# The output gates of a hybrid encoder kernel: GpSimd taken out, bound and negation on VectorE, three ScalarE functions in a row

## The chip, the cores and the metric

The kernel runs on one core of one Trainium2 chip. Its time is the device time of one execution in microseconds (us); runs are compared by their median. TensorE (PE) multiplies matrices, VectorE (DVE) and ScalarE (ACT) work on tiles of 128 partitions, GpSimd (POOL) is the fourth compute engine, and SyncE (SP) issues the transfers. Each engine works its own list of instructions in order; semaphores make it wait for the others.

## The reference, cut to what matters

Two layers of an encoder run over 272 positions (256 tokens and 16 meta tokens) of width 2048. Each layer has one wide input projection, a bidirectional gated linear attention (GLA) with 4 heads, a neighbourhood attention (NA) with 16 heads, an output projection and a squared-ReLU MLP. The part that matters here is the output gate of the GLA heads: a quarter of the projection's GLA columns, `r`, goes through `silu` and multiplies the normalised attention output.

```python
    o = o * lax.rsqrt(jnp.mean(jnp.square(o), axis=-1, keepdims=True) + LN_EPS) * norm_w.astype(f32)
    o = o.reshape(B, L, GLA_HEADS * GLA_DV) * jax.nn.silu(r.astype(f32))
    return o.astype(q.dtype)
```

`silu(r)` is r / (1 + exp(-r)).

## The kernel before, in words

Activations lie transposed: a tile has 128 features on the partitions and the positions along the free side (272 in layer 0; the last layer needs 256 for the gates). Every product is made of fp32r parts. A weight chunk of 128x1024 lands in `raw`, ScalarE rounds it to `wh` (L165), VectorE forms the rest `wl` = raw - wh (L166), and TensorE multiplies wh and wl with the high and low halves of the activations: three matmuls of 272 columns for each of 16 row blocks in layer 0 (L178, L179, L180), or a 512- and a 256-column one in layer 1 (L174, L175). So a gate tile takes 48 matmuls in layer 0 and 32 in layer 1. Three chunk buffers are in turn, and the chunks of the whole kernel stream through them.

`by_m` runs one output tile after the other: it fills a PSUM bank `mm`, hands it to an eviction function, and calls `pump` twice a tile. Where the bank holds 256 + 256 columns (layer 1), `whole` first joins the two halves into the SBUF tile `jn` (a ScalarE copy, L187, and a VectorE add, L188), and the eviction reads that.

`pump` moves side work along. Side work stands in two queues of Python generators, `fg` and `bg`; a step runs a generator up to its next `yield`, and its VectorE instructions may not stand ahead of the newest `wl`. In the gate stage each pump gives one step of `fg` and 1.3 of `bg`. In `bg` are the four GLA heads. A head has nine levels of scores: VectorE forms `dif` (L494), ScalarE takes exponentials into `lev` (L496, L498), VectorE multiplies by q and k (L499), TensorE makes the scores into a bank `bg` (L520), VectorE merges them by a mask (L527). Then follow one more product (L535), the product with V (L553 to L557), a mean of squares (L560, L227, L791), its Newton step, and at the end the output `on`, which is multiplied by the gate tiles (L572, L573) and split into `y`. In `fg` are the gates' later steps and, from the next stage on, the NA pairs (scores L613, transposes L649, outputs L664).

The order on each engine is laid down by the tile framework's scheduler when the program is built: it takes instructions by priority when its own model of time says they are ready, so a change of one instruction can move others. That order is fixed before the run.

The gates: `ev_r` evicts each of 8 gate tiles a layer. ScalarE writes exp(-r) from the bank into `rs` (L442); GpSimd adds one (L443); ScalarE writes -r into `rv` (L445). The generator `silu` then lets two steps pass, takes Ln and Exp (L454, L455) in its third, which gives a first value of 1 / (1 + exp(-r)), and at the next VectorE does one Newton step and the product (L457, L458, L459). `rs` and `rv` have two buffers each. A head's end waits until its two gate tiles are there.

Of the kernel before, what the change touches and what calls it, by code (L numbers as in the profile page):

```python
# [10 lines left out]
AF = mybir.ActivationFunctionType  # L11
ALU = mybir.AluOpType
# [41 lines left out]
class Trunk:  # L54
# [382 lines left out]
    def ev_r(self, c, ps):  # L437

        nc, n = self.nc, self.n
        self.y[c] = self.pair(self.yp, "y", c)  # L440
        s = self.g2.tile([P, L], F32, name="rs", tag="rs")[:, :n]
        nc.scalar.activation(s, ps, AF.Exp, scale=-1.0)  # L442
        nc.gpsimd.tensor_scalar(s, s, 1.0, 1.0, ALU.mult, ALU.add)  # L443
        r = self.g2.tile([P, L], F32, name="rv", tag="rv")[:, :n]
        nc.scalar.mul(r, ps, -1.0)  # L445
        self.fg.append(self.silu(c, s, r))

    def silu(self, c, s, r):
        nc = self.nc
        stt = nc.vector.scalar_tensor_tensor  # L450
        yield
        yield
        gate = self.g2.tile([P, L], F32, name=f"gate{c}", tag=f"gate{c}", bufs=1)[:, :self.n]
        nc.scalar.activation(gate, s, AF.Ln)  # L454
        nc.scalar.activation(gate, gate, AF.Exp, scale=-1.0)  # L455
        yield
        stt(s, s, 1e30, gate, ALU.min, ALU.mult)  # L457
        stt(s, s, 2.0, gate, ALU.subtract, ALU.mult)  # L458
        nc.vector.tensor_tensor(gate, r, s, ALU.mult)  # L459
        self.gate[c] = gate  # L460
# [692 lines left out]
```

## Time and profile before

| | us |
|---|---|
| median of 3 runs (2367.51 to 2368.08) | 2367.93 |
| the profiled execution: its time | 2367.06 |
| the profiled execution: its span, first to last instruction | 2365.3 |
| gate stage of layer 0, first and last L442 | 117.2, 170.5 |
| gate stage of layer 1, first and last L442 | 1326.2, 1380.3 |

The profile is that of one execution. An engine's busy time is the time in which it has an instruction in work; an idle stretch is put down to what came last before it ended. In rows of a window, x is the number of instructions; in rows of the timeline, the columns are start, duration, engine, line, operation, output and input, and in brackets the idle time just before and what ended it.

### The profile page before, as it was taken

Reading aid. Unit: us, or ns where it says so; the run is one execution under the profiler, and the core shown is the slowest. Engines: PE = TensorE matmul, PEld = TensorE weight load, DVE = VectorE, ACT = ScalarE, POOL = GpSimd, SP = SyncE. Lnnn points to the kernel's source line nnn. Section 1 sums busy time; section 2 is a strip of 40 time slices with the busy share of each in tenths; the row PEclk is TensorE's granted clock in tenths of the full one; section 3 lists DMA queues with packets and bytes.
Section 4 is the critical chain, followed back from the end, with each engine's and each line's share of the span. In section 5 each row is a group of like instructions: output and inputs, shape, how many; then the busy total and the mean of one; then the engine's idle time right before and its main releaser. Section 6 shows DMA issues by size and latency. Waiting matters only on the chain.

```text
span 2365.3 us, 43178 instructions
## 1 busy us (share of the span) xinstructions
PE 2340.4 (99%) x17354; PEld 2228.3 (94%) x17354; DVE 1568.2 (66%) x2458; ACT 1240.6 (52%) x2267; POOL 124.5 (5%) x197
## 2 busy tenths in 40 slices
PE   9999999999999999999999999999999999999997
PEld 9999999999999999999999899998988888888887
DVE  6687777785544455547577887768866555666656
ACT  6566665564433344444456767655654333444444
POOL 1110000020000000000021010000200000000001
PEclk9999999999999999999999999999999999999999
DMA  7544445555555555555555454546566666666664
GB/s 250 167 140 143 140 145 160 179 179 179 179 180 182 182 179 178 180 180 178 180 179 182 151 158 144 154 152 202 185 194 195 193 193 194 196 192 193 195 192 138
DMA packets 120424, 417.47 MB, mean 177 GB/s; under 512 B 13404, under 2 KB 18396, under 8 KB 120224
## 3 DMA queue, kind: packets, MB, share of 16 engines
q1 hardware_dynamic: 120224, 414.72, 56.1%
q8 instruction: 136, 2.23, 0.4%
q14 instruction: 64, 0.52, 0.1%
HBM read 412.57 MB, written 2.10 MB: 175 GB/s over the span
## 4 chain that ended last, share of the span: by engine, by line
PE 93%; DVE 4%; issue 1%; ACT 1%; POOL 0%; DMA 0%; SPq 0%; ACTq 0%; DVEq 0%; POOLq 0%
PE mm L174 21%; PE mm L178 17%; PE mm L179 17%; PE mm L180 17%; PE mm L175 11%; PE mm L204 6%; PE bg L520 1%; DVE wl L166 1%; PE bg L664 1%; ACT wh L165 0%; PE bg L613 0%; PE bg L351 0%; PE mm L946 0%; PE bg L553 0%; PE mm L961 0%
## 5 line engine op out<-in xcount | busy, mean ns | idle before, releaser
L166 DVE TENSOR_TENSOR wl<-raw,wh 128x1024 fp32r<-128x1024 f32 (+1 forms) x764 | 931.6, 1220 | 642.3 <-ACT wh L165 629.4
L165 ACT CAST wh<-raw 128x1024 fp32r<-128x1024 f32 (+1 forms) x764 | 796.4, 1042 | 926.6 <-PE mm L179 368.5
L178 PE MATMUL mm<-x,wh 128*128 128x272 f32 (+2 forms) x2176 | 622.4, 286 | 0.0
L179 PE MATMUL mm<-x,wh 128*128 128x272 f32 (+2 forms) x2176 | 617.9, 284 | 0.0
L180 PE MATMUL mm<-x,wl 128*128 128x272 f32 (+2 forms) x2176 | 617.0, 284 | 0.1
L179 PEld LDWEIGHTS mm<-x,wh 128*128 128x128 f32 x2176 | 408.7, 188 | 0.1
L178 PEld LDWEIGHTS mm<-x,wh 128*128 128x128 f32 x2176 | 407.6, 187 | 1.1 <-issue 0.5
L180 PEld LDWEIGHTS mm<-x,wl 128*128 128x128 f32 x2176 | 407.2, 187 | 0.5 <-DVE wl L166 0.5
L174 PE MATMUL mm<-x,wh 128*128 128x512 f32 x1152 | 397.6, 391 | 0.0
L175 PE MATMUL mm<-x,wl 128*128 128x256 f32 x1152 | 318.1, 276 | 0.0
L174 PEld LDWEIGHTS mm<-x,wh 128*128 128x128 f32 x1152 | 216.3, 188 | 45.0 <-issue 0.6
L174 PE MATMUL mm<-y,wh 128*128 128x512 f32 x672 | 230.3, 388 | 0.0
L175 PEld LDWEIGHTS mm<-x,wl 128*128 128x128 f32 x1152 | 216.2, 188 | 0.0
L178 PE MATMUL mm<-y,wh 128*128 128x272 f32 x704 | 199.2, 283 | 0.0
L179 PE MATMUL mm<-y,wh 128*128 128x272 f32 x704 | 199.2, 283 | 0.0
L180 PE MATMUL mm<-y,wl 128*128 128x272 f32 x704 | 199.0, 283 | 0.0
L175 PE MATMUL mm<-y,wl 128*128 128x256 f32 x672 | 184.6, 275 | 0.7 <-DVE wl L166 0.7
L174 PE MATMUL mm<-u,wh 128*128 128x512 f32 x480 | 164.7, 388 | 0.0
L174 PEld LDWEIGHTS mm<-y,wh 128*128 128x128 f32 x672 | 126.0, 188 | 26.0 <-ACT wh L165 0.2
L178 PE MATMUL mm<-u,wh 128*128 128x272 f32 x512 | 144.9, 283 | 0.0
L179 PE MATMUL mm<-u,wh 128*128 128x272 f32 x512 | 144.9, 283 | 0.0
L180 PE MATMUL mm<-u,wl 128*128 128x272 f32 x512 | 144.7, 283 | 0.0
(264 smaller groups left out, 3285.5 us busy)
## 6 DMA issues: line engine op xcount, KB each, us to landing
raw<-in_wff SPq DMA_DIRECT2D x512, 512.0 KB, 3.5
raw<-in_win SPq DMA_DIRECT2D x190, 512.0 KB, 3.6
raw<-in_wout SPq DMA_DIRECT2D x64, 512.0 KB, 3.5
nb<-in_nab SPq DMA_DIRECT2D x16, 352.0 KB, 3.5
xraw<-in_xT SPq DMA_DIRECT2D x7, 272.0 KB, 5.1
out<-acc SPq DMA_DIRECT2D x7, 256.0 KB, 2.4
wraw<-in_wup SPq DMA_DIRECT2D x2, 392.0 KB
raw<-in_win SPq DMA_DIRECT2D x4, 128.0 KB, 2.7
```

The lines of the kernel that those rows point to most:

```text
L165: nc.scalar.copy(wh[:, c], raw[:, c])
L166: self.wl = nc.vector.tensor_tensor(wl[:, c], raw[:, c], wh[:, c].bitcast(F32), ALU.subtract).ins
L174: mm(ps, lhsT=wh[:, c:c + P], rhs=x.joined, start=first, stop=False)
L175: mm(ps[:, T:], lhsT=wl[:, c:c + P], rhs=xh[:, :T], start=False, stop=last)
L178: mm(o, lhsT=wh[:, c:c + P], rhs=xh[:, :n], start=first, stop=False)
L179: mm(o, lhsT=wh[:, c:c + P], rhs=xl[:, :n], start=False, stop=False)
L180: mm(o, lhsT=wl[:, c:c + P], rhs=xh[:, :n], start=False, stop=last)
L204: self.nc.tensor.matmul(ps[m][:, :n], lhsT=parts[p][0][:, c:c + P], rhs=acts[j][parts[p][1]][:, :n], start=j + p == 0, stop=j == nk - 1 an ...
L520: nc.tensor.matmul(ps[:, b], lhsT=k[:, b], rhs=q[:, r], start=True, stop=True)
L664: nc.tensor.matmul(r[hs], lhsT=(v2 if rest else v1)[:, t, hs], rhs=p2[:, t, :] if rest else p1[:, 2 * t + hh, :], start=rest, stop=not rest)
```

## The change

```diff
@@ ev_r
         s = self.g2.tile([P, L], F32, name="rs", tag="rs")[:, :n]
-        nc.scalar.activation(s, ps, AF.Exp, scale=-1.0)
-        nc.gpsimd.tensor_scalar(s, s, 1.0, 1.0, ALU.mult, ALU.add)
         r = self.g2.tile([P, L], F32, name="rv", tag="rv")[:, :n]
-        nc.scalar.mul(r, ps, -1.0)
+        nc.vector.tensor_scalar(r, ps, -1.0, 85.0, ALU.mult, ALU.min)
+        nc.scalar.activation(s, r, AF.Exp)
         self.fg.append(self.silu(c, s, r))
@@ silu
-        yield
-        yield
         gate = self.g2.tile([P, L], F32, name=f"gate{c}", tag=f"gate{c}", bufs=1)[:, :self.n]
-        nc.scalar.activation(gate, s, AF.Ln)
+        nc.scalar.activation(gate, s, AF.Ln, bias=self.one)
         nc.scalar.activation(gate, gate, AF.Exp, scale=-1.0)
         yield
-        stt(s, s, 1e30, gate, ALU.min, ALU.mult)
+        stt(s, s, 1.0, gate, ALU.add, ALU.mult)
         stt(s, s, 2.0, gate, ALU.subtract, ALU.mult)
         nc.vector.tensor_tensor(gate, r, s, ALU.mult)
```

VectorE now evicts the tile: it negates r and bounds it at 85 (L443 of the changed file), from the bank in layer 0 and from `jn` in layer 1. ScalarE takes exp of that (L444), then Ln with a bias of one (L451), then Exp (L452). The Newton step adds the one itself (L454 to L456). A gate takes one step of `fg` where it took three, two of them empty; its VectorE part runs at the start of the step that follows. From L445 of the old file on, a line has a number lower by 3 in the changed one: L520 is L517, L499 is L496, L494 is L491.

The first place is in layer 0, after the sixth gate tile, where head 0 ends and head 1 forms its first level. VectorE before (`on` and `y` end head 0; `dif`, `lev` with `_85`, `_81` belong to head 1):

```order
L573 TENSOR_TENSOR on<-on,gate_1617 128x272
L573 TENSOR_TENSOR on<-on,gate_1771 128x272
L166 TENSOR_TENSOR wl<-raw,wh 128x1024
L227 TENSOR_TENSOR y_1518<-on,y_1518 128x272
L227 TENSOR_TENSOR y_1611<-on,y_1611 128x272
L494 TENSOR_TENSOR dif<-be_85 128x2x256
L166 TENSOR_TENSOR wl<-raw,wh 128x1024
L499 TENSOR_TENSOR lev<-lev,qk_81 128x2x256
```

VectorE now, at the same place:

```order
L570 TENSOR_TENSOR on<-on,gate_1523 128x272
L570 TENSOR_TENSOR on<-on,gate_1621 128x272
L454 SCALAR_TENSOR_TENSOR rs<-rs,gate_2017 128x272
L227 TENSOR_TENSOR y_1518<-on,y_1518 128x272
L455 SCALAR_TENSOR_TENSOR rs<-rs,gate_2017 128x272
L227 TENSOR_TENSOR y_1616<-on,y_1616 128x272
L456 TENSOR_TENSOR gate_2017<-rv,rs 128x272
L166 TENSOR_TENSOR wl<-raw,wh 128x1024
L491 TENSOR_TENSOR dif<-be_85 128x2x256
L166 TENSOR_TENSOR wl<-raw,wh 128x1024
L443 TENSOR_SCALAR rv<-mm 128x272
L496 TENSOR_TENSOR lev<-lev,qk_81 128x2x256
```

The three gate operations of the sixth tile, which stood behind this `lev`, are ahead of it, and so is the eviction of the seventh tile; the eviction of the sixth (another L443) stands three rows above the piece. ScalarE at that place, before:

```order
L442 ACTIVATE rs<-mm 128x272
L445 ACTIVATE rv<-mm 128x272
L454 ACTIVATE gate_2371<-rs 128x272
L226 CAST y_1518<-on 128x272
L226 CAST y_1611<-on 128x272
L455 ACTIVATE gate_2371<-gate_2371 128x272
L165 CAST wh<-raw 128x1024
```

ScalarE now:

```order
L444 ACTIVATE rs<-rv 128x272
L451 ACTIVATE gate_2017<-rs,one 128x272
L452 ACTIVATE gate_2017<-gate_2017 128x272
L226 CAST y_1518<-on 128x272
L226 CAST y_1616<-on 128x272
L165 CAST wh<-raw 128x1024
```

The second read of the bank is gone, and the three functions follow each other. On TensorE the scores that use this `lev` stood two matmuls into the eighth gate tile and now stand 16 into it, so 14 matmuls later.

The second place is the same one in layer 1. TensorE before (x_13030 is the fourth row block of the eighth gate tile; L520 with `qk` is the diagonal level):

```order
L174 MATMUL mm<-x_12989,wh 128x512
L175 MATMUL mm<-x_12989,wl 128x256
L174 MATMUL mm<-x_13030,wh 128x512
L520 MATMUL bg<-lev 128x128 x2
L520 MATMUL bg<-lev,qk_14504 128x128 x2
L175 MATMUL mm<-x_13030,wl 128x256
```

TensorE now (x_13559 is the ninth row block):

```order
L174 MATMUL mm<-x_13427,wh 128x512
L175 MATMUL mm<-x_13427,wl 128x256
L174 MATMUL mm<-x_13559,wh 128x512
L517 MATMUL bg<-lev 128x128 x2
L517 MATMUL bg<-lev,qk_14496 128x128 x2
L175 MATMUL mm<-x_13559,wl 128x256
```

Head 1's first scores of layer 1 stand 10 matmuls later, its next levels 10 to 24 later; from head 2 on most of them are where they were. Elsewhere, the first NA pair of each layer starts two tiles (96 matmuls in layer 0) earlier, since `fg` is empty sooner, the next pairs by less, and the fifth where it did.

## The prediction

> **What bounds the kernel now.** I read the busy times and the chain of the page first, then the windows around the two gate stages, then each wait of TensorE in them.
>
> ```profile
> span 2365.3 us, 43178 instructions
> ...
> PE 2340.4 (99%) x17354; PEld 2228.3 (94%) x17354; DVE 1568.2 (66%) x2458; ACT 1240.6 (52%) x2267; POOL 124.5 (5%) x197
> ...
> PE 93%; DVE 4%; issue 1%; ACT 1%; POOL 0%; DMA 0%; SPq 0%; ACTq 0%; DVEq 0%; POOLq 0%
> ```
>
> TensorE is busy for 2340.4 of 2365.3 us, and it is 93% of the chain that ends last. The change takes no matmul away and adds none. So it can only move the 24.9 us in which TensorE has nothing, and of these only the part that lies where the change reaches: the gate stages (112 to 200 and 1314 to 1400 us) and the NA stages behind them.
>
> In such a row stand the window and its length, the busy time and count of PE, PEld, DVE, ACT and POOL, the granted clock, the DMA share and GB/s.
>
> ```profile
> 112.00:200.00 88.00, 86.51 (x685) 84.44 (x685) 71.69 (x128) 57.41 (x137) 10.59 (x15) 1.00 0.47 144
> 200.00:362.00 162.00, 161.67 (x1393) 156.86 (x1393) 123.43 (x269) 108.06 (x321) 15.44 (x28) 1.00 0.46 142
> 1314.00:1400.00 86.00, 84.64 (x540) 75.45 (x539) 77.38 (x143) 63.49 (x159) 10.08 (x15) 1.00 0.48 150
> 1400.00:1556.00 156.00, 155.41 (x1214) 144.61 (x1213) 117.56 (x210) 104.89 (x294) 12.81 (x28) 1.00 0.49 150
> ```
>
> Window less PE busy is 1.49, 0.33, 1.36 and 0.59 us: 3.77 us in all. A gain of more than 0.2% of 2367.93 us, which is 4.74 us and about what a measurement of this kernel can tell from no change, is more than all of it. The granted clock is 1.00 in each of these windows. VectorE is the engine with the least room there.
>
> These are the waits of TensorE in them, one row each:
>
> ```profile
> 151.06 0.87 PE L791 MATMUL bg<-sp,onesr 128*128 128x272 f32 x2 [0.26 <-ACT sp L226]
> 162.00 0.68 PE L520 MATMUL bg<-lev 128*128 128x128 f32 x4 [1.02 <-DVE lev L499]
> 1323.87 0.71 PE L520 MATMUL bg<-lev 128*128 128x128 f32 x4 [0.40 <-DVE lev L499]
> 1332.53 0.46 PE L520 MATMUL bg<-lev 128*128 128x128 f32 x2 [0.24 <-DVE lev L499]
> 1366.82 0.46 PE L520 MATMUL bg<-lev 128*128 128x128 f32 x2 [0.72 <-DVE lev L499]
> 1416.28 0.49 PE L520 MATMUL bg<-lev 128*128 128x128 f32 x2 [0.21 <-DVE lev L499]
> ```
>
> All but the first wait for a `lev` of VectorE. The change gives VectorE more to do, so each has to be worked out by itself.
>
> **What is removed.** GpSimd's addition and ScalarE's second read of the bank:
>
> ```profile
> L443 POOL TENSOR_SCALAR rs<-rs x16: 406/814/1473, 117.6 to 1380.8; 128x272 f32<-128x272 f32 x8, 128x256 f32<-128x256 f32 x8
> ...
>   ACT gate L454: 5.0, 9
> ...
> L445 ACT ACTIVATE rv<-mm x8: 387/388/405, 117.5 to 170.8; 128x272 f32<-128x272 f32 x8
> L445 ACT ACTIVATE rv<-jn x8: 400/401/410, 1326.6 to 1380.6; 128x256 f32<-128x256 f32 x8
> ```
>
> The 16 additions take 0.41 to 1.47 us, and ScalarE stood for 5.0 us in 9 of them. With 8 x 0.39 + 8 x 0.40 = 6.3 us of L445 that is 11.3 us of ScalarE, 5.6 us a layer. ScalarE isn't full (57.41 of 88, 63.49 of 86), so this is worth something only where a `lev` or an `sp` waited for it. The bias of one in Ln and the one in the Newton step change no count of instructions.
>
> **What is added:** 16 evictions on VectorE. No row before shows a one-input operation of this size with a bound, so I go by the nearest rows:
>
> ```profile
> L368 DVE SCALAR_TENSOR_TENSOR gt<-bg,gt 128x272 f32<-128x272 f32 x16 | 7.1, 441 | 2.5 <-ACT gt L367 1.8
> L407 DVE COPY V<-bg 128x128 f32<-128x128 f32 x32 | 7.6, 285 | 10.5 <-PE bg L404 10.4
> L188 DVE TENSOR_TENSOR jn<-jn,mm 128x256 f32<-128x256 f32 x72 | 29.8, 413 | 1.4 <-ACT jn L187 1.4
> L344 DVE TENSOR_SCALAR wraw<-wraw,sel 98x1024 f32<-98x1024 f32 x2 | 1.5, 748 | 0.0
> L995 DVE TENSOR_SCALAR acc<-acc,vec 128x128 f32<-128x128 f32 x2 | 0.6, 342 | 0.0
> ```
>
> From a bank of 272 columns: between 0.285 us (a copy of 128) and 0.441 us; I take 0.44, the row of the same size. From `jn`, 256 columns in SBUF: 0.41 us at most, the row of the same shape, and at least 748 x 256 / 1024 = 0.19 us from L344; L995, the same kind of operation, takes 0.34 for half as many columns, so I take 0.41. Together 8 x 0.44 + 8 x 0.41 = 6.8 us (4 to 7), in stages where VectorE works 71.69 of 88 and 77.38 of 86 us.
>
> L344 takes 0.73 ns an element where a two-input operation like L188 takes 1.6. The Trainium skill's page "VectorE: DVE Perf Modes" (section "The perf-mode tier table") says that a one-source fp32 operation runs two elements a cycle between SBUF tiles and one from PSUM. By that rule layer 1's eviction would take some 0.29 us, an estimate from the page's 150 cycles plus 128 at 0.96 GHz, and the two places of layer 1 below would cost 0.2 to 0.4 us less; L344's row leans that way, L995's does not.
>
> **What is moved:** a gate's VectorE operations (three of 0.42 to 0.44 us) come ahead of scores that they stood behind, and TensorE's order puts these scores off. How long a matmul is there:
>
> ```profile
> 60.00:74.00 14.00, 10.52 (x38) 6.94 (x38) 1.00 0.56 183
> 1720.00:1800.00 80.00, 80.00 (x236) 44.16 (x236) 1.00 0.64 196
> ```
>
> The first row is L178 alone, one of three, so 14 / 114 = 0.123 us a matmul in layer 0; the second L174 alone, one of a pair, so 80 / 472 = 0.17 us in layer 1.
>
> *Layer 0, 162.00.* The wait of 1.02 us, with its chain:
>
> ```profile
> 157.67 0.43 ACT L454 ACTIVATE gate<-rs 128x272 f32<-128x272 f32 x1 [1.26 <-POOL rs L443]
> 158.44 0.80 DVE L227 TENSOR_TENSOR y<-on,y 128x272 fp32r<-128x272 f32 x2 [1.08 <-ACT y L226]
> 160.03 1.22 DVE L166 TENSOR_TENSOR wl<-raw,wh 128x1024 fp32r<-128x1024 f32 x1 [0.19 <-ACT wh L165]
> 161.17 0.68 DVE L499 TENSOR_TENSOR lev<-lev,qk 128x512 f32<-128x512 f32 x1
> ```
>
> GpSimd holds ScalarE for 1.26 us; the casts of `y` and the next `wh` stand behind it, and VectorE idles 1.08 + 0.19 = 1.27 us for them. `lev` is done at 161.85; TensorE was there at 160.98. After the change that idle time goes, and two evictions (0.88) and three gate operations (1.29) are new ahead of `lev`: 161.85 - 1.27 + 2.17 = 162.75. TensorE arrives 14 x 0.123 = 1.72 us later, at 162.70. The wait falls to about 0.1: **-0.9 us**.
>
> *Layer 0, 151.06.*
>
> ```profile
> 148.29 0.43 ACT L454 ACTIVATE gate<-rs 128x272 f32<-128x272 f32 x1 [0.98 <-POOL rs L443]
> ```
>
> Ahead of `sp` ScalarE stood 0.98 us for GpSimd. That is more than the 0.26 us: **-0.26**. What is late next there is VectorE's gate work ahead of the squares, which the 0.98 us covers.
>
> *Layer 1, 1366.82.*
>
> ```profile
> 1364.86 1.21 DVE L166 TENSOR_TENSOR wl<-raw,wh 128x1024 fp32r<-128x1024 f32 x1
> 1365.99 0.68 DVE L499 TENSOR_TENSOR lev<-lev,qk 128x512 f32<-128x512 f32 x1
> 1366.60 0.40 DVE L188 TENSOR_TENSOR jn<-jn,mm 128x256 f32<-128x256 f32 x1
> 1366.93 0.68 DVE L494 TENSOR_TENSOR dif<-be 128x512 f32<-128x512 f32 x1
> ```
>
> VectorE has no idle time here to win back. Operations follow each other a little before the last ends (1366.60 to 1366.93, 0.33 us for one of 0.40). Ahead of this `lev` come two evictions, three gate operations and the join that stood behind it, 6 x 0.33 = 2.0 us; TensorE comes 10 x 0.17 = 1.7 us later. **+0.3 us**, between -0.3 (evictions of 0.19) and +0.7 (no overlap). *1332.53* is alike: five operations, 1.65 us, against nine matmuls, 1.5 us: **+0.1**. *1323.87* lies before the first eviction: 0.
>
> *Layer 1, end of head 0.* The chunk that TensorE needs just before the product with V:
>
> ```profile
> 1339.78 0.42 DVE L188 TENSOR_TENSOR jn<-jn,mm 128x256 f32<-128x256 f32 x1 [0.39 <-ACT jn L187]
> 1346.37 2.56 DVE L166 TENSOR_TENSOR wl<-raw,wh 128x1024 fp32r<-128x1024 f32 x2
> 1351.37 0.59 PE L553 MATMUL bg<-A,V 128*128 128x256 f32 x2
> ```
>
> The first of the two L166 is ready at about 1347.65 and used 14 matmuls ahead of L553, 1351.37 - 2.4 = 1349.0: 1.35 us to spare. Four evictions and three gate operations come ahead of it, 7 x 0.33 = 2.3 us, less the 0.39 us that VectorE idled on the way: up to 0.6 us late, or not at all if the evictions are short. I take the middle, **+0.3**.
>
> *NA pairs earlier.*
>
> ```profile
> 162.00:182.00 20.00, 20.00 (x166) 19.98 (x167) 19.36 (x38) 12.67 (x32) 1.87 (x2) 1.00 0.50 149
> 192.00:202.00 10.00, 10.00 (x77) 9.69 (x76) 4.42 (x6) 4.78 (x8) 1.47 (x3) 1.00 0.51 158
> 1326.00:1382.00 56.00, 55.04 (x338) 48.61 (x337) 53.62 (x94) 42.94 (x108) 7.47 (x10) 1.00 0.50 160
> 1396.00:1406.00 10.00, 10.00 (x70) 9.40 (x69) 4.43 (x7) 5.53 (x10) 0.50 (x3) 1.00 0.47 142
> ```
>
> The rows of 192 and 1396 are where the first pair goes, those of 162 and 1326 what it leaves alone: it moves into the stretches where VectorE works only 4.4 of 10 us, and out of the one around 1416: **-0.2**. Its bias transfers move on SP's queue past three or four weight chunks; the DMA share is 0.47 to 0.51, so I cost that at nothing. Were a chunk wanted at that moment, one transfer of 128x704 floats (0.36 MB) at 151 GB/s would hold it 2.4 us.
>
> The sum: -0.9 - 0.26 + 0.3 + 0.1 + 0.3 - 0.2 = -0.7 us. Against the profiled execution, 2367.06 us (span 2365.3 and 1.8 around it), that is 2366.4; that execution is 0.9 under the median of the runs shown, so for a median I take 2367.93 - 0.7 = **2367.2 us**.
>
> **Rivals.** *VectorE becomes the bound* (slower). In 1326 to 1382 it works 53.62 of 56 us. Evictions bring 8 x 0.41 = 3.3, and six gate operations that now run behind 1382 come in, 2.5: 59.4, so 3.4 us over; in layer 0 the row from 162 to 182 has 19.36 of 20, and three evictions make it 0.7 over. If TensorE's later order covers nothing, it waits 4.1 us more, and nothing of the old waits goes: 2372.0, and 2374.4 with a chunk late as well. It decides from the point where VectorE's added time ahead of a `lev` is more than the matmuls by which its scores are put off. For it: 96% busy. Against it: the put-off of 10 to 24 matmuls, 1.7 to 4.1 us, is of the size of the added work, and behind 1396 there is room. In the Trainium skill, "Perfetto Trace Analysis" (section "Optimizing Scalar/DVE Operations") speaks for this rival: where VectorE is saturated, work should go from it to ScalarE or even GpSimd, and this change goes the other way. Chance 0.15, a third of it over 4.74 us.
>
> *All waits of the gate stages go* (faster, yet hardly to be told): VectorE's evictions are as short as 0.19 us in layer 1 and the freed ScalarE is never late; then 1.49 + 1.36 = 2.85 us go: 2365.1. Waits under 0.16 us don't show as idle time, since a matmul lasts 0.28 and the next starts after 0.12; they could add 1 to 2 us. For it: the 5.0 us of ScalarE. Against it: three of the five waits of these stages have VectorE behind them, not GpSimd. Chance 0.18, with 0.02 past 4.74 us.
>
> **How the numbers follow.** The forecast (2366 to 2369) has 0.67, the two rivals 0.15 and 0.18. A range of 2365.0 to 2370.8 takes in all waits gone at the low end and most of VectorE's overflow at the high end. Faster by over 0.2% 0.02, within 0.2% 0.93, slower 0.05.
>
> **What would show it.** Right: L520 near 162 waits under 0.3 us, L791 near 151 not at all; GpSimd's busy time falls by about 14 us (16 x 0.8); VectorE's rises by 4 to 7; in layer 1 the first scores of head 1 still wait, 0.5 to 1.4 us. Wrong: TensorE idle by over 3 us in 1314 to 1400, a `wl` among its waits there (VectorE the bound), or evictions that idle VectorE because they stand before their bank is full.

## The result, and the profile after

| | us |
|---|---|
| before, median of 22 runs (2367.04 to 2368.77) | 2367.78 |
| changed, median of 22 runs (2363.86 to 2365.56) | 2364.94 |
| ratio, 95% interval | 0.9987 (0.9982 to 0.9993) |
| profiled execution of the changed kernel: its time, its span | 2365.56, 2363.8 |

The change gains 2.84 us, 0.12%: within 0.2%, as forecast, but four times the 0.7 us forecast and just beyond the low end of the range, 2365.0. The interval leaves out 1, so here 0.12% can be told from no change; the 0.2% that the prediction took for the limit was too wide. The profiled execution is the slowest of the 22, and so the two profiles lie only 1.50 us apart (spans of 2365.3 and 2363.8) where the medians lie 2.84 apart.

The page of the changed kernel: span, busy times, and shares of the chain that ends last.

```profile
span 2363.8 us, 43168 instructions
...
PE 2339.4 (99%) x17354; PEld 2228.2 (94%) x17354; DVE 1570.9 (66%) x2474; ACT 1239.3 (52%) x2251; POOL 109.8 (5%) x181
...
PE 95%; DVE 3%; ACT 1%; issue 1%; DMA 0%; SPq 0%; ACTq 0%; DVEq 0%
```

GpSimd lost 14.7 us and TensorE has as many matmuls as before. VectorE's busy time rose by only 2.7 us. The same windows as before, with the columns of the prediction:

```profile
112.00:200.00 88.00, 87.53 (x705) 86.02 (x703) 76.75 (x148) 60.08 (x141) 3.83 (x7) 1.00 0.49 148
200.00:362.00 162.00, 161.64 (x1397) 157.57 (x1396) 122.17 (x263) 105.99 (x311) 15.38 (x30) 1.00 0.46 142
1314.00:1400.00 86.00, 85.46 (x542) 75.61 (x540) 80.12 (x155) 63.53 (x159) 2.96 (x7) 1.00 0.49 156
1400.00:1556.00 156.00, 155.68 (x1220) 145.58 (x1219) 117.14 (x207) 103.20 (x288) 11.27 (x30) 1.00 0.49 148
```

Window less PE busy is now 0.47, 0.36, 0.54 and 0.32 us: 1.69 us, where it was 3.77. Both gate stages gained, layer 1's as well (1.36 to 0.54), for which the forecast had a loss. Two later profiles of the same kernel have 0.94 and 0.78 us in layer 1's window, since a matmul near 1354 waits 0.41 and 0.24 us for `sp` there and not in the first profile; the fall of idle time in layer 1 is thus 0.42 to 0.82 us. Two of the waits that are left, and the evictions with who waited for them:

```profile
162.12 0.68 PE L517 MATMUL bg<-lev 128*128 128x128 f32 x4 [0.34 <-DVE lev L496]
...
1321.52 0.71 PE L517 MATMUL bg<-lev 128*128 128x128 f32 x4 [0.41 <-DVE lev L496]
```

```profile
L443 DVE TENSOR_SCALAR rv<-mm x8: 422/433/442, 116.8 to 168.1; 128x272 f32<-128x272 f32 x8
L443 DVE TENSOR_SCALAR rv<-jn x8: 281/286/294, 1324.4 to 1372.4; 128x256 f32<-128x256 f32 x8
...
  ACT rs L444: 3.2, 4
```

The first score of that row waits 0.34 us where it waited 1.02. The waits near 151 and 1366 us are gone, and the one at 1321 us, ahead of the first gate tile, stands as it stood. An eviction takes 0.43 us from a bank and 0.29 us from `jn`.

### The profile page after: what moved, and what is told of

It is laid out like the page before. It is cut to its first block, busy times and chain, and to the rows that moved or that the text cites. A ratio compares the mean times of both kernels' runs of the same rounds, so it can differ in the third digit from the quotient of the medians.

```text
span 2363.8 us, 43168 instructions
## 1 busy us (share of the span) xinstructions
PE 2339.4 (99%) x17354; PEld 2228.2 (94%) x17354; DVE 1570.9 (66%) x2474; ACT 1239.3 (52%) x2251; POOL 109.8 (5%) x181
## 4 chain that ended last, share of the span: by engine, by line
PE 95%; DVE 3%; ACT 1%; issue 1%; DMA 0%; SPq 0%; ACTq 0%; DVEq 0%
PE mm L174 21%; PE mm L178 17%; PE mm L179 17%; PE mm L180 17%; PE mm L175 11%; PE mm L204 6%; PE bg L517 2%; PE bg L661 1%; DVE wl L166 1%; PE bg L610 0%; ACT wh L165 0%; PE bg L550 0%; PE bg L351 0%; PE mm L943 0%; PE mm L958 0%
## 5 line engine op out<-in xcount | busy, mean ns | idle before, releaser
L166 DVE TENSOR_TENSOR wl<-raw,wh 128x1024 fp32r<-128x1024 f32 (+1 forms) x764 | 931.2, 1219 | 638.0 <-ACT wh L165 625.8
```

What stands on the lines that cost most here:

```text
L166: self.wl = nc.vector.tensor_tensor(wl[:, c], raw[:, c], wh[:, c].bitcast(F32), ALU.subtract).ins
```

## The experiments

Three theories were put to the test. A: GpSimd's addition inside ScalarE's chain was what cost. B: the two empty steps taken out of `silu` give a better order. C: ScalarE's second read of the bank was what cost. Each kernel was timed beside the kernel before on its chip; the three groups ran on different chips, so a gain is given against the median of before in its own group.

| run | us, median | against before of its group |
|---|---|---|
| group 1, before | 2367.91 | |
| before without the two steps | 2375.47 | +7.56, ratio 1.0030 (1.0019 to 1.0042) |
| changed, two steps put back | 2364.34 | -3.57, ratio 0.9983 (0.9974 to 0.9992) |
| before, bias instead of GpSimd | 2364.65 | -3.26, ratio 0.9986 (0.9977 to 0.9995) |
| the same without the two steps | 2364.72 | -3.19, ratio 0.9986 (0.9977 to 0.9994) |
| group 2, before | 2367.43 | |
| changed, GpSimd put back | 2373.33 | +5.90, ratio 1.0027 (1.0016 to 1.0038) |
| bias, GpSimd aside | 2365.95 | -1.48, ratio 0.9994 (0.9985 to 1.0003) |
| before, addition on VectorE | 2364.34 | -3.09, ratio 0.9987 (0.9978 to 0.9996) |
| changed again | 2364.66 | -2.77, ratio 0.9990 (0.9981 to 0.9999) |
| group 3, before | 2369.30 | |
| bias, GpSimd aside twice | 2367.23 | -2.07, ratio 0.9992 (0.9983 to 1.0001) |
| bias again | 2364.90 | -4.40, ratio 0.9983 (0.9974 to 0.9992) |
| steps put back, again | 2364.31 | -4.99, ratio 0.9980 (0.9971 to 0.9989) |
| changed, third time | 2365.39 | -3.91, ratio 0.9984 (0.9975 to 0.9992) |

In group 3 the kernel before spread from 2367.31 to 2371.24; there the kernels are compared with each other.

### The two steps alone

```diff
@@ silu, of the kernel before
         stt = nc.vector.scalar_tensor_tensor
-        yield
-        yield
```

> The kernel before with one thing changed: the two empty steps of a gate are gone, so a gate's Ln comes two steps earlier and the NA pairs start earlier; GpSimd still adds the one and ScalarE still reads the bank twice. Theory A (GpSimd's addition inside ScalarE's chain was what cost): Ln comes closer behind the addition, ScalarE's idle time before it grows from 5.0 us to 8 or more, and the time is 0 to 1 us over that of the kernel before. Theory B (the order that follows from the two steps brings the gain): 1.5 to 2.8 us under it. Theory C (the second read of the bank by ScalarE was what cost): within 0.4 us of it.

It is 7.56 us slower. Its windows of the two gate stages, then its row of GpSimd's additions and the ScalarE instructions that waited for them (time, times):

```profile
112.00:200.00 88.00, 83.59 (x667) 81.29 (x666) 70.73 (x133) 55.14 (x133) 12.45 (x14) 1.00 0.43 134
...
1314.00:1400.00 86.00, 81.18 (x519) 71.59 (x518) 75.60 (x141) 61.03 (x154) 11.28 (x12) 1.00 0.44 140
```

```profile
L443 POOL TENSOR_SCALAR rs<-rs x16: 404/1156/2074, 118.1 to 1381.1; 128x272 f32<-128x272 f32 x8, 128x256 f32<-128x256 f32 x8
...
  ACT gate L452: 13.0, 12
```

TensorE idles 4.41 and 4.82 us in the two windows, 6.38 more than before. Without the steps Ln comes right behind the addition, and ScalarE stands for 13.0 us instead of 5.0. Theory B falls in its plain form: the new order by itself, with GpSimd still in the chain, is the dearest single edit of the study. Theory A has the sign and the mechanism, but allowed one microsecond only.

### The two steps put back into the changed kernel

```diff
@@ silu, of the changed kernel
         stt = nc.vector.scalar_tensor_tensor
+        yield
+        yield
```

> The changed kernel with the two empty steps of a gate put back; VectorE bounds and negates, GpSimd has nothing to do in a gate. Theory A: 2.2 to 3 us under the kernel before, the wait at 162 us under 0.4 us and none at 151 us. Theory B: within 1 us of the kernel before, with waits of 0.2 us at 1416 us again. Theory C: 2.2 to 3 us under, as A.

As A and C expected, and a little more: 3.57 us under the kernel before. TensorE idles 0.11 and 0.41 us in the gate stages. Whatever the gain is, it doesn't need the removed steps.

### The bias alone, and the bias with the steps removed

```diff
@@ ev_r and silu, of the kernel before
         nc.scalar.activation(s, ps, AF.Exp, scale=-1.0)
-        nc.gpsimd.tensor_scalar(s, s, 1.0, 1.0, ALU.mult, ALU.add)
...
-        nc.scalar.activation(gate, s, AF.Ln)
+        nc.scalar.activation(gate, s, AF.Ln, bias=self.one)
...
-        stt(s, s, 1e30, gate, ALU.min, ALU.mult)
+        stt(s, s, 1.0, gate, ALU.add, ALU.mult)
```

> The kernel before without GpSimd's addition and nothing else: ScalarE writes exp(-r) and -r from the bank as before, Ln takes the one as its bias, the Newton step adds it (its bound of 1e30 is left out), the two empty steps stay. Theory A: 2 to 3 us under the kernel before. Theory B: 0 to 0.5 us under. Theory C: 0 to 0.7 us under, since ScalarE keeps both reads.

> The same as the run with the bias alone, and the two empty steps removed too, so that only VectorE's evictions of the changed kernel are missing (the bound of 1e30 is left out here as well). Theory A: 2 to 3 us under the kernel before, as with the bias alone. Theory B: 1.5 to 2.8 us under. Theory C: 0 to 1 us under. If VectorE's evictions cost time where VectorE is full (layer 1), this one is under the changed kernel.

Both have the whole gain (-3.26 and -3.19 us, a little over the 3 that A allowed) with ScalarE's two bank reads still there, so C falls as its cause, and neither VectorE's evictions nor the removed steps are needed for it. With the steps left in, the evictions add a little: the kernel that has them is 0.31 us under the one with the bias alone here, and 0.59 us in the third group (2364.31 and 2364.90), though the ranges overlap. In the kernel with the bias alone all but 46 of the 17354 matmuls of TensorE's order, and all of SyncE's transfers, stand where they stood before:

```profile
112.00:200.00 88.00, 87.85 (x699) 86.02 (x698) 72.28 (x131) 59.25 (x138) 2.79 (x7) 1.00 0.48 144
...
1314.00:1400.00 86.00, 85.53 (x547) 76.54 (x546) 76.53 (x143) 64.94 (x160) 3.12 (x7) 1.00 0.50 154
```

Idle time falls to 0.15 and 0.47 us there. This pair of kernels also tells how much the rows of idle time leave out. From one matmul of V's transposes ahead of each gate stage to the corresponding NA score behind it, layer 0 shrinks from 182.80 to 181.09 us and layer 1 from 225.33 to 224.21 us: 2.83 us, while idle time in the four windows falls from 3.77 to 1.55, by 2.22 us. The 0.6 us between them lie for the most part in the very waits that the rows show. Around 151 us the starts of the same matmuls come 0.67 us earlier, for a row of 0.26; around 1332 us 0.47 for 0.24; around 1366 us 0.88 for 0.72. In layer 0 a matmul's record lasts 0.28 us where the next may start after 0.12, so the first 0.16 us of a wait can stand as busy time.

### GpSimd put back into the changed kernel

```diff
@@ ev_r and silu, of the changed kernel
         nc.scalar.activation(s, r, AF.Exp)
+        nc.gpsimd.tensor_scalar(s, s, 1.0, 1.0, ALU.mult, ALU.add)
...
-        nc.scalar.activation(gate, s, AF.Ln, bias=self.one)
+        nc.scalar.activation(gate, s, AF.Ln)
...
-        stt(s, s, 1.0, gate, ALU.add, ALU.mult)
+        stt(s, s, 1e30, gate, ALU.min, ALU.mult)
```

> The changed kernel with GpSimd's addition of one put back between ScalarE's Exp and Ln (no bias, the bound of 1e30 again); VectorE evicts, the two empty steps stay out. In ten of the sixteen gates Ln is now the next or the next but one on ScalarE behind that Exp. Theory A (ScalarE waits for GpSimd in the middle of its chain): ScalarE's idle time before Ln is 12 us or more, and the time 6 to 12 us over the kernel before, as much as without the two steps there or more. Theory B (the order brings the gain) is already against the runs; it would give about the changed kernel's time. Theory C (ScalarE's second read of the bank): no more than 1 us over the changed kernel.

It is 5.90 us over the kernel before, 0.1 less than the least that A expected. What ScalarE's Ln waited for in it:

```profile
  POOL rs L445: 14.6, 15
```

Fifteen of sixteen gates stand, 14.6 us in all. This one edit undone costs 8.7 us against the changed kernel of the same group (2373.33 less 2364.66).

### GpSimd aside, and twice

Is the cost ScalarE's wait, or GpSimd's operation as such? Here it works on `rv`, which no one needs until the gate's last product. In the second kernel the added line stands twice.

```diff
@@ ev_r, of the kernel with the bias alone
         nc.scalar.mul(r, ps, -1.0)
+        nc.gpsimd.tensor_scalar(r, r, 1.0, 0.0, ALU.mult, ALU.add)
```

> The kernel with the bias alone (2364.65 us), and GpSimd multiplies rv by one in place (16 operations of the size of its additions) where no one waits for it before the gate's last product, several us later. The bound of 1e30 is left out. Two readings of theory A: A1, ScalarE's wait in the chain is the whole cost: within 0.5 us of the kernel with the bias alone, GpSimd's operations as long as before (0.4 to 1.5 us). A2, GpSimd's operation itself holds up VectorE beside it: 1 to 3 us over the kernel with the bias alone, and VectorE's operations beside it longer by 0.2 us or more each.

> As the run with GpSimd aside, but with two such operations in a row in each gate, 32 in all; no one waits for them before the gate's last product. A1 (only ScalarE's wait in the chain costs): within 0.7 us of the kernel with the bias alone. A2 (GpSimd's operations hold up VectorE's operations beside them): the cost of one such operation a gate, 1.3 to 1.8 us by the runs so far, about doubles: 2.5 to 4 us over the kernel with the bias alone on this chip, so about the time of the kernel before.

One operation a gate costs 1.3 us against the kernel with the bias alone (2365.95 and 2364.65, two groups; 1.8 by their gains). Two cost 2.33 us on the same chip (2367.23 and 2364.90), a little under the 2.5 expected. So GpSimd costs something even where no one waits for it. The place near 160 us shows how. First VectorE, GpSimd and TensorE with GpSimd aside (start, duration), then VectorE at the same place with the bias alone:

```profile
155.78 1.43 DVE L166 TENSOR_TENSOR wl<-raw,wh 128x1024 fp32r<-128x1024 f32 x1
157.13 0.99 DVE L227 TENSOR_TENSOR y<-on,y 128x272 fp32r<-128x272 f32 x2
...
155.46 0.68 POOL L445 TENSOR_SCALAR rv<-rv 128x272 f32<-128x272 f32 x1 [7.10 <-ACT rv L444]
156.11 1.38 POOL L485 TENSOR_SCALAR lev<-qk 128x272 f32<-128x272 f32 x1
...
160.61 0.68 PE L520 MATMUL bg<-lev 128*128 128x128 f32 x4 [0.68 <-DVE lev L499]
```

```profile
156.30 1.22 DVE L166 TENSOR_TENSOR wl<-raw,wh 128x1024 fp32r<-128x1024 f32 x1
157.44 0.79 DVE L227 TENSOR_TENSOR y<-on,y 128x272 fp32r<-128x272 f32 x2
```

Beside the two GpSimd operations VectorE's L166 and one of the two L227 take 0.2 us longer each, and that lands on the next `lev`. Counted over both gate stages, VectorE operations that ran over 0.12 us longer than the median of their kind are 1 with the bias alone, 6 before (1.23 us), 9 with GpSimd aside (1.76 us) and 15 with it twice (3.01 us). All those in the kernels with GpSimd's work have two inputs in SBUF; L188, with one of its two in PSUM, keeps its 0.40 to 0.42 us throughout. In the Trainium skill, "SBUF — State Buffer" (section "Who interferes with whom") has this: a VectorE instruction with two SBUF inputs contends with a GpSimd instruction that reads SBUF, since its second input comes over the read interface that both share. The trace agrees, at 0.13 to 0.25 us for each such operation of VectorE. GpSimd's side pays more: its operation takes 0.41 us at best and up to 1.56 us with GpSimd aside, up to 3.55 us where two stand in a row.

So A2 holds, and A1, that ScalarE's wait is the whole cost, does not; but the wait is the larger part. At 2.33 us of time for 3.01 us of stretched operations, the 1.23 us of before are worth some 1 us; that is an estimate. By difference the other 2 us or so of the 3.26 are ScalarE's wait. With GpSimd aside, where the wait is gone and GpSimd's operations are not, 1.48 us were gained. No run has the wait without the stretching.

### The addition on VectorE

```diff
@@ ev_r, of the kernel before
-        nc.gpsimd.tensor_scalar(s, s, 1.0, 1.0, ALU.mult, ALU.add)
+        nc.vector.tensor_scalar(s, s, 1.0, 1.0, ALU.mult, ALU.add)
```

> The kernel before with the addition of one on VectorE instead of GpSimd, at the same place in ScalarE's chain, and nothing else. A1a (any other engine in the chain costs, since VectorE's list in order puts the addition behind its other work): 0 to 3 us over the kernel before, ScalarE idle before Ln for 5 us or more. A1b (it was GpSimd's slow addition, 0.41 to 1.47 us against about 0.3 us on VectorE): 1.5 to 3 us under the kernel before, ScalarE idle before Ln for under 2 us.

The whole gain again, 3.09 us, just over what A1b gave, with an engine still in the middle of ScalarE's chain. The operation's durations in this kernel (least, median, most), and ScalarE's wait for it:

```profile
L443 DVE TENSOR_SCALAR rs<-rs x16: 282/294/491, 118.2 to 1382.5; 128x272 f32<-128x272 f32 x8, 128x256 f32<-128x256 f32 x8
...
  ACT gate L454: 0.8, 3
```

VectorE does in 0.29 us what took GpSimd 0.81, and ScalarE waits 0.8 us instead of 5.0. It was the slow addition, not the hand-over. This kernel is also rid of the stretching: no two-input operation of VectorE but one runs over 0.12 us longer than its kind.

### The changed kernel again, and what the steps still cost

> The changed kernel unaltered, for a second profile and its time beside the others: 2364.4 to 2365.6 us. If the waits at 10.5 us and 1599 us are those of one execution (transfers), they differ by more than 0.3 us here; if they belong to the change, they are the same within 0.2 us. The waits of the gate stages are the same in either case.

> The kernel with the bias alone, unaltered, as the base on this chip: 3 to 3.5 us under the kernel before, TensorE idle under 0.3 us in 112 to 200 us, no wait at 1599 us.

> The changed kernel with the two empty steps put back, unaltered, beside the changed kernel on the same chip: 0.4 to 1 us under it, if the wait of 0.7 to 1.1 us near 1599 us belongs to the removed steps (it stood in all five profiles without them and in none of the five with them).

> The changed kernel unaltered, on the same chip: 2.7 to 3 us under the kernel before, the waits near 1599 us (0.7 to 1.1) and 10.5 us (0.9) there again if they belong to this program and not to one execution.

On one chip the changed kernel with the steps put back takes 2364.31 us (2363.63 to 2365.10) and the changed kernel 2365.39 (2364.58 to 2365.74): 1.08 us apart, a little over what was expected. With the steps it is under both kernels that were given; the addition on VectorE, on another chip, is as fast (2364.34). Against before, the bias (-4.40) and the changed kernel (-3.91) are beyond what was expected in this group, since before's median is 2369.30 in it. The changed kernel's second time is as expected, but not its waits in the gate stages: layer 1's differ, as said with the result. Most of the 1.08 us is near 1599 us. Two windows, of the kernel with the steps and of the one without:

```profile
1590.00:1610.00 20.00, 19.35 (x112) 16.45 (x111) 20.00 (x47) 11.97 (x21) 0.00 (x0) 1.00 0.50 158
```

```profile
1590.00:1610.00 20.00, 18.60 (x107) 15.79 (x106) 19.25 (x46) 11.11 (x19) 0.00 (x0) 1.00 0.52 152
```

The second is the changed kernel's first profile: 1.40 us idle against 0.65. Over all profiles, the six without the steps idle 1.05 to 1.80 us there, the eight with them 0.65 to 0.66. In the changed kernel's third profile it looks like this:

```profile
1593.20 0.33 SPq L164 DMA_DIRECT2D raw<-in_wout  x1
...
1598.16 1.05 ACT L165 CAST wh<-raw 128x1024 fp32r<-128x1024 f32 x1 [3.81 <-DMA raw<-in_wout]
...
1599.26 0.50 PE L174 MATMUL mm<-y,wh 128*128 128x512 f32 x1 [0.54 <-ACT wh L165]
```

and with the steps put back, at the same place of the program:

```profile
1593.58 0.33 SPq L164 DMA_DIRECT2D raw<-in_wout  x1
...
1597.16 1.05 ACT L165 CAST wh<-raw 128x1024 fp32r<-128x1024 f32 x1 [2.44 <-DMA raw<-in_wout]
```

From issue to cast it is 4.96 us against 3.58, for the same chunk. Over all profiles it is 4.79 to 5.54 us in the six without the steps and 3.46 to 3.60 in the eight with them. By the rule that was set for the second profile, a difference of over 0.3 us would have made it an accident of one execution, and the idle time does differ by 0.40 (1.40 and 1.80); but the wait is there each time, so it goes with the removed steps.

The NA bias transfers, which the removed steps also move, can't stand in this chunk's way: the last of them is issued near 1510 us in these kernels, over 80 us earlier. What differs beside the chunk is another transfer, of 16 KB, on a queue that the page calls `instruction`. The packets, MB and share of each queue from the chunk's issue to its landing, without the steps (1593.20 to 1598.06) and with them (1593.58 to 1597.06):

```profile
q1 hardware_dynamic: 239, 0.90, 57.1%
q8 instruction: 1, 0.02, 1.4%
```

```profile
q1 hardware_dynamic: 153, 0.56, 60.4%
```

In the six profiles without the steps this transfer starts 1.1 to 2.1 us after the chunk's issue, and the chunk lands after 4.7 to 5.4 us. In the eight with them it starts after 3.2 to 4.9 us, when the chunk is landing or has landed (3.4 to 3.5 us); then the next chunk is the slow one, with 4.1 to 5.0 us, and no idle row of TensorE follows. Over a whole profile, chunks that have such a transfer beside them take 3.9 to 4.6 us from issue to landing (medians of the 14 profiles), the others 3.5 to 3.6. So with the steps removed this transfer falls beside a chunk that TensorE needs at once. The two go together in all 14 profiles; no run moved that transfer alone.

The wait at 10.5 us does not hold up in the same way: it is 0.99, 0.88 and 0.29 us in the changed kernel's three profiles, but also 0.36 in one of the two with the bias alone, and none in the other, and 0.32 with GpSimd aside. So it changes from execution to execution of one kernel. Its cause stays open; the gates come a hundred microseconds later.

## Why the prediction was off

**What bounds the kernel: right in kind, short in amount.** The change moved only waits of TensorE. But the sum took the rows of idle time for all that could be won ("it can only move the 24.9 us in which TensorE has nothing") and left what a row doesn't show to a rival. A better measure is the time at which two kernels have done the same matmuls. By it the changed kernel's three profiles gain 2.77, 2.77 and 2.78 us from 111.9 to 361.9 us of before, in layer 0. Idle time falls by only 0.98 or 0.99 there, and only 1.82 us of it had stood there. In layer 1 (1320.0 to 1589.8) they gain 0.89, 0.53 and 0.71 us, and by 1610 they have lost 0.88, 1.24 and 0.66 again, at the late chunk, which lies behind the stages that the prediction looked at. The forecast was -1.16 us for layer 0, +0.5 for layer 1 (its three places and the -0.2 of the NA pairs) and nothing for the late chunk.

**162.00 and 151.06: right in mechanism, too small.** The forecast had -0.9 and -0.26 us with GpSimd's wait as the cause; the first fell from 1.02 to 0.34, the second is gone. By the starts of the same matmuls, 1.63 us were gained from 149.9 to 164.9 us, not 1.16: a row shows less than the whole of a wait. The kernel with the bias alone, with neither of these waits left, shows that the cause was the right one.

**Layer 1: wrong, and this is the step that failed.** It was costed at +0.3, +0.1 and +0.3 us, so +0.7; idle time there fell by 0.42 to 0.82. Three things are in it. First, the sentence "VectorE has no idle time here to win back": it had, inside its operations. Ahead of the wait at 1366.82, before:

```profile
1362.04 1.42 DVE L166 TENSOR_TENSOR wl<-raw,wh 128x1024 fp32r<-128x1024 f32 x1
1363.38 0.94 DVE L227 TENSOR_TENSOR y<-on,y 128x256 fp32r<-128x256 f32 x2
...
1361.99 0.41 POOL L443 TENSOR_SCALAR rs<-rs 128x256 f32<-128x256 f32 x1 [6.57 <-ACT rs L442]
1362.36 1.37 POOL L485 TENSOR_SCALAR lev<-qk 128x256 f32<-128x256 f32 x1
```

and with the bias alone:

```profile
1360.03 1.22 DVE L166 TENSOR_TENSOR wl<-raw,wh 128x1024 fp32r<-128x1024 f32 x1
1361.17 0.75 DVE L227 TENSOR_TENSOR y<-on,y 128x256 fp32r<-128x256 f32 x2
...
1363.58 0.68 DVE L498 TENSOR_TENSOR lev<-lev,qk 128x512 f32<-128x512 f32 x1
```

From this L166 to `lev` it is 3.55 us where it was 3.95. GpSimd's L485 stood behind the addition, which had waited 6.57 us for ScalarE, and so came beside L166 and L227; without the addition it runs 10 us earlier. L166 and one L227 took 0.2 us longer each: 0.4 of the 0.72 us. In that kernel the whole wait is gone, so the rest came with the earlier start of the chain. Second, the evictions from `jn`: 0.41 us was taken, from a row with two inputs, and 0.286 measured. The estimate by the Trainium skill's page "VectorE: DVE Perf Modes" (section "The perf-mode tier table"), 0.29 us, was right, and L344's row, which leaned that way, was the one to follow. Third, the work that moved ahead of `lev`, put at 2.0 us. The stretch from the join to `lev` in the changed kernel:

```profile
1358.74 0.42 DVE L188 TENSOR_TENSOR jn<-jn,mm 128x256 f32<-128x256 f32 x1
...
1365.06 0.68 DVE L496 TENSOR_TENSOR lev<-lev,qk 128x512 f32<-128x512 f32 x1
```

It is 6.32 us, against 1365.99 less 1361.04, the same join's start before, 4.95 us: 1.37 us more, not 2.0. TensorE's put-off covers it. Nor did a `wl` come late at the end of head 0, which was the last +0.3: the only new wait there is the one for `sp` near 1354, in two profiles of three.

**NA pairs earlier, -0.2: right where it looked, outweighed elsewhere.** The wait near 1416 went and one of 0.23 us at 1404 came. A wait of 0.33 us at 1496, in a window that the prediction shows but not in its list of waits, went too:

```profile
1496.30 0.68 PE L520 MATMUL bg<-lev 128*128 128x128 f32 x4 [0.33 <-DVE lev L499]
```

By the same matmuls, from 111.9 to 1589.8 us, removing the steps gains about 1 us where the bias replaces GpSimd (3.8 against 2.7) and nothing beside VectorE's evictions (3.2 to 3.6 against 3.4). The late chunk then costs 0.7 to 1.2 us. So with the bias alone the steps change nothing that can be measured (2364.65 and 2364.72), and in the changed kernel they cost about a microsecond. That they would cost 7.6 us as long as GpSimd stayed was seen nowhere in the prediction, which took the parts one by one.

**The bias in Ln** was costed at nothing in time. It is not quite nothing, and a row of before had it: L367, a Ln with a bias tile.

```profile
L367 ACT ACTIVATE gt<-gt,one x16: 522/523/524, 49.2 to 1301.8; 128x272 f32<-128x272 f32 x16
```

The gate's Ln went from 0.42 to 0.51 us; ScalarE has room, and no one waits for it.

**The rivals.** "VectorE becomes the bound" did not come, at 80.12 of 86 us busy. "All waits of the gate stages go" was the nearest, at 2365.1; it fell short of all of them, and what the rows leave out came on top. That is 1.6 to 1.7 us up to 1590 in the three profiles of the changed kernel (3.66 us gained for 2.08 of idle time in the first), in the 1 to 2 us that it allowed. For "VectorE becomes the bound" the prediction names the Trainium skill's page "Perfetto Trace Analysis" (section "Optimizing Scalar/DVE Operations"). The Trainium skill says there only that such a move off a saturated VectorE "may make sense", and warns that between VectorE and GpSimd it might not help. Here the opposite move, GpSimd's addition to VectorE, gained 3.09 us.

**What would show it.** GpSimd fell by 14.7 us (14 forecast, though 16 x 0.8 is 12.8) and L791 near 151 no longer waits. The wait near 162 is 0.34, not under 0.3. VectorE rose by 2.7 us, not 4 to 7: 8 x 0.43 + 8 x 0.29 = 5.8 us are new, and the durations of all its operations add up to 5.4 us more, but the page counts time in which two overlap once. The first scores of head 1 in layer 1, which were to wait 0.5 to 1.4 us, don't wait.

## What to carry to other kernels

A slow engine costs twice where its work is small: the engine that waits for it stands still, and VectorE's two-input operations beside it grow longer without any idle time. Look for operations that run longer than their kind before writing that an engine has nothing to win back. And test the parts of a change apart and together: here the step removal alone cost 7.6 us, the bias alone gave the whole gain, and the moved evictions gave 0.3 and 0.6 us on two chips. Compare the starts of the same matmuls in two traces, too: rows of idle time left out some 1.6 us of what the changed kernel gained in its stages.

## What the chip showed that was not expected

GpSimd's addition of a gate tile took 0.40 to 2.11 us over these runs, five times its least; in the kernel before it took 0.41 or 0.42 us in the four places with little or no two-input work of VectorE beside it, and 0.41 to 1.47 us beside such work. On VectorE it took 0.28 to 0.49 us. A chunk of 512 KB took 1.4 us longer from issue to use (4.96 against 3.58), at the same place of the program, with only the two steps between the kernels: a 16 KB transfer on the `instruction` queue had come beside it.
